# A hybrid decoder layer on one core: one more pair of up columns and two more down tiles by half products, raw chunks asked for one pair earlier, compression blocks laid out contiguously

## The chip, the cores and the metric

One core of a Trainium2 chip runs the whole layer as one program. The metric is the device time of one execution in microseconds, as the median of several runs. A difference under 0.3% is about what a measurement of this kernel cannot tell from no change.

## The reference, cut to what matters

One decoder layer on 512 tokens of width 1024, in float32:

```python
h = rms_norm(x, mix_norm_g)
u, q, kv, nsa_g, merge_g = split(h @ w_in)
y_pool = pooling_mixer(u) @ w_pool_out          # windowed means of widths 2, 4, 8, 16
# compress_blocks: 31 blocks of 32 tokens, stride 16, for k and for v
blk = kv[:, idx] + pe
hid = silu(einsum('bnlgd,ldh->bngh', blk, w1)); kc = einsum('bngh,hd->bngd', hid, w2)
y_nsa = nsa_mixer(q, kv, ...) @ w_nsa_out       # compressed, selected and window attention
x = x + (gate_pool * y_pool + gate_nsa * y_nsa) @ w_out
h = rms_norm(x, ffn_norm_g)
gate_pre, val = split(h @ w_up)                 # 1024 -> 2 * 2816
x = x + (silu(causal_dwconv(gate_pre) + b) * val) @ w_down
```

The width 2816 is 22 tiles of 128 columns. Pair f below means tile f of gate and tile f of value.

## The kernel before, in words

**Numbers.** Every matrix product is made of three matmuls: a float32 operand is split into a high part (rounded to fp32r by ScalarE) and a low part (the rest), and high·high, high·low and low·high are summed in PSUM. Two kinds of split exist: `split` (ScalarE rounds, VectorE subtracts) and `split_by_dma` (ScalarE writes the negative, a DMA issued by GpSimd adds the raw values onto it, ScalarE rounds). The latter's transfers are called accumulates here; they are the rows `sl<-r`, `sl<-s`, `sl<-wraw`, `wlo<-wraw`, `tl<-tb`.

**Stages.** First q, k (`round_a`), then attention (stream `m`) with the feature products, pooling and pool_out (stream `f`) put between its matmuls; then `wno`, `out` (8 outputs `x2[f]`), and the feed-forward part. In attention's stage the compressed keys and values are made: for k and v, GpSimd adds the position terms (`kcb`), the sum is split into `kcs`, and 32 matmuls `tr<-w1s,kcs` multiply 16 block offsets by `w1`. Offset l of the 32 takes every eighth element of `kcs` as its stationary operand.

**Feed-forward.** Pairs 0 to 3 (`PLAIN = 4`) are plain: 2 x 8 x 3 matmuls with 512 columns. Pairs 4 to 21 go by half products: `seven` makes seven operands from four raw quarters of the two weight tiles (a11, a12 and five sums h1 to h5), and seven products of 4 x 3 matmuls with 256 columns each (`product`) take the place of eight. The moving side needs sums too: `halves` makes `nh`, `nl`, `th`, `tl` from `x2` once, after pair 0. A pair leaves its last two products (h5, h4) to be done after a11 of the next pair (`held`). Between the products stand pieces of the down product: groups of four y tiles (`dn_group`, started at the pairs in `AT`, handed out by `FILL`). One piece is 4 x 3 matmuls of 512 columns. The last six y tiles (16 to 21) are multiplied by half products at the end: four row pairs (`seven_into`, called dz below), 7 x 3 x 3 matmuls each, whose moving operands `zh`, `zl` are sums of y tiles (`sums_of`).

**What sets the order.** Everything is recorded as operations with dependencies; a planner (`Plan.run`) gives each engine an order by costs and due times, tries several and keeps the best by its own `TRIALS`. Engines then work through their orders strictly. 56 pages of 512 columns hold most tiles. Pages taken by `soon` (raw chunks r1 and r2, the sums s3, the halves sh and sl) are given in a fixed sequence, the order in which the program asks for them, and such a page is taken only if `AHEAD` pages are free. Weight chunks go through a ring of three `wraw` buffers. SyncE (SP) issues all loads, GpSimd (POOL) all accumulates.

Nearly all instructions are recorded at one helper line (L398), so rows are told apart by tile names.

Of the kernel before, what the change touches and what calls it, by code (L numbers as in the profile page):

```python
# [15 lines left out]
P = 128  # L16
# [29 lines left out]
_o = 0  # L46
for _n, _w in (("ident", 128), ("mask", 512), ("cmask", 128), ("valid", 4), ("recip", 64), ("inv", 8)):
# [12 lines left out]
TRIES = 12  # L60
# [51 lines left out]
class Plan:  # L112
# [116 lines left out]

    def run(self, key, reserve, land, rate=RATE, fixed=None):  # L230
        ops = self.ops
# [33 lines left out]
        def settle(limit):  # L265
            while True:
                act = [l for l in queue.values() if l and l[0][0] <= now[0]]
                t = min((l[0][0] for l in queue.values() if l and l[0][0] > now[0]), default=1e18)
                head = None
                if act:  # L270
                    l = min(act, key=lambda l: l[0][1])
                    if now[0] + l[0][1] * len(act) <= t:
                        t, head = now[0] + l[0][1] * len(act), l
                if t > limit:
                    return False
                for l in act:
                    l[0][1] -= (t - now[0]) / len(act)
                now[0] = t
                if head:
                    o = head.pop(0)[2]  # L280
                    o.fin = t + land
                    finish(o)
                    return True
# [95 lines left out]
    def emit(self, tries, reserve):  # L379
# [8 lines left out]
        for i in range(tries):  # L388
# [3 lines left out]
            fixed = {e: [o for o in order if o.eng == e] for e in ("PE", "ACT", "DVE", "POOL", "SP")}  # L392
            spans = sum(self.run(key, 0, land, rate, fixed)[1] for land, rate in TRIALS)
            if best is None or spans < best[0]:
# [7 lines left out]
def hybrid_layer(ctx: ExitStack, tc: tile.TileContext, first, xT, pos, par, cst, poolw, w1, wa, wb, wf,  # L402
# [162 lines left out]
    for k in range(KD):  # L565
# [180 lines left out]
    with pl.on("f"):  # L746
        for i in range(2):
# [6 lines left out]
            for a in range(2):  # L754
                b = page("kcb", (P, 2, 32, 8))
                POOL.tensor_add(b.rearrange("p g n l -> p (g n) l"), kc.rearrange("p g (n l) -> p (g n) l", l=8),
                                pe[:, i, 8 * a:8 * a + 8][:, None, :].to_broadcast([P, 64, 8]))
                KC[i, a] = pl.tile(sb, (P, 2, T), F32R, "kcs", ("ptc", "t_cst")[a], 1)
                split(KC[i, a][:, 0], KC[i, a][:, 1], b.rearrange("p g n l -> p (g n l)"))
        def pool_in(gi):  # L760
# [82 lines left out]
    for i in range(2):  # L843
# [264 lines left out]

    def seven(w, row, first, second, when):
        rg, r1, r2 = ring("wraw")[:, :2 * w], soon("r1")[:, :w], soon("r2")[:, :w]  # L1110
        SP.dma_start(rg, row)
        with pl.behind(*when):
            SP.dma_start(r1, first)
            SP.dma_start(r2, second)

        def pair():
# [6 lines left out]

        a1 = ring("whi", F32R)[:, :2 * w], ring("wlo", F32R)[:, :2 * w]
        split(*a1, rg)
        s3 = soon("s3")[:, :w]
        DVE.tensor_add(s3, rg[:, :w], r1)
        h5 = summed(r2)
        DVE.tensor_add(r1, r1, r2)
        h3 = summed(s3)  # L1130
        DVE.tensor_add(rg[:, :w], rg[:, :w], r1)
        h1 = summed(r1)
        h2 = pair()
        split(*h2, rg[:, :w])
        DVE.tensor_add(rg[:, w:], rg[:, w:], rg[:, :w])
        h4 = summed(rg[:, w:])
        return [tuple(q[:, i * w:(i + 1) * w] for q in a1) for i in range(2)] + [h1, h2, h3, h4, h5]

    def seven_into(o0, o1, w, mv, nk, done, last):
# [11 lines left out]
        def rest():  # L1151
            bq = any_bank()
            product(bq, h1, mv(2, 0), True, nk)
            add(o1, HI, bq, -1)
            product(bx, a12, mv(1, 0), False, nk)
            add(o0, LO, bx, 1)
            product(by, h2, mv(2, 1), False, nk)
            add(o0, HI, by, 1)
            product(bq, h4, mv(1, 1), False, nk)
            add(o0, HI, bq, 1)  # L1160
            done(0)
            product(by, h3, mv(3, 0), False, nk)
            add(o1, HI, by, -1)
            done(1)

            def end():
                product(by, h5, mv(3, 1), False, nk)
                add(o1, LO, by, -1)
                done(2)

# [29 lines left out]
    def take(f):  # L1200
# [20 lines left out]

    turn[0] = 16
# [4 lines left out]
    tt = [pl.tile(sb, (P, 2, T), F32R, "th", "ptc", 1)]   # L1227
    tt = [tt[0][:, k] for k in range(2)] + [page("th", dt=F32R) for _ in range(2)]
    t2 = pl.tile(sb, (P, 2, T), F32R, "th", "t_cst", 1)
    t2 = [t2[:, k] for k in range(2)] + [page("th", dt=F32R)]  # L1230
    t3 = [pl.tile(sb, (P, T), F32R, n, "t_" + n, 1) for n in ("oraw", "ot")]
# [25 lines left out]
    zh, zl, ylast = {}, {}, {}  # L1257

    def split_y(f, y):
        yh[f], yl[f] = page("yh", dt=F32R), page("yl", dt=F32R)  # L1260
        split(yh[f], yl[f], y)
        if f < 16:
            return
        ylast[f] = y
        if f % 2:
            k = (f - 16) // 2
            for i, x in enumerate(sums_of(ylast[f - 1], y)):
# [49 lines left out]
    def dn_group(g):  # L1317
        box = {}

        def load(c):  # L1320
            box[c] = weights(wdn[g, c].rearrange("p a k n -> p (a k n)"), 1024, "v")

        def part(pt, c, a, k0, k1):
            wh, wl = box[c]
            s = slice(a * 512, (a + 1) * 512)
            mm3(pt, wh[:, s], wl[:, s], yh, yl, 4 * g + k0, 4 * g + k1, koff=4 * g, nk=4 * g + 4, first=4 * g)

        def one(c, a, free):
            if a == 0:
                load(c)  # L1330
            pt = any_bank() if free else bank("sc", (P, 2, T))[:, 0]
            part(pt, c, a, 0, 4)
            DVE.tensor_add(x2[2 * c + a], pt, x2[2 * c + a])

        def both(free):
            load(0)
            pts = any_bank(), any_bank()
            for k0, k1 in ((0, 3), (3, 4)):
                for a in range(2):
# [9 lines left out]

    def up_fast(f, n1, n2, n3):  # L1350
        a11, a12, h1, h2, h3, h4, h5 = seven(512, flat(wup[f, 0]), flat(wup[f, 1, :, 0:4]), flat(wup[f, 1, :, 4:8]),
                                             begun[-2:-1])
        bx, by, bq = any_bank(), any_bank(), any_bank()
# [50 lines left out]
    fill(9, True)  # L1404
    def put(j, p):
        f = 2 * p + (j > 0)
        if p < 3 or j == 0:
            if j != 1:
                SP.dma_start(out[f], x2[f])
        else:  # L1410
            c = LO if j > 1 else HI
            SP.dma_start(out[f, :, c], x2[f][:, c])

    last = None
    for p in range(4):
        w7 = seven(384, flat(wdz[2 * p]), flat(wdz[2 * p + 1, :, 0:3]), flat(wdz[2 * p + 1, :, 3:6]), begun[-1:])
        last = seven_into(x2[2 * p], x2[2 * p + 1], w7, movy, 3, lambda j, p=p: put(j, p), last)
    last()
# [7 lines left out]
def _layout(x, positions, mix_norm_g, w_in, q_norm_g, k_norm_g, cmp_pe, cmp_w1, cmp_w2, pool_w,  # L1426
# [65 lines left out]
    wd = tiles(f(w_down)[0])  # L1492
    A["wdn"] = wd[:, :, :16].reshape(4, 2, P, 4, 4, P).transpose(3, 0, 2, 1, 4, 5)
    A["wdz"] = wd[:, :, [16, 18, 20, 17, 19, 21]]
    return {n_: np.ascontiguousarray(A[n_]) for n_ in _INS}
# [19 lines left out]
```

## Time and profile before

| | us |
|---|---|
| median of 3 runs (lowest to highest) | 691.58 (690.17 to 692.01) |
| the profiled execution | 692.38 |
| its span | 689.9 |
| TensorE busy | 681.9 (99%) |
| VectorE busy | 508.6 (74%) |
| ScalarE busy | 445.4 (65%) |
| GpSimd busy | 115.9 (17%) |

The span runs from the first to the last instruction of the profiled execution; 2.44 us of its time lie around it. Matmuls overlap in the records (one of 512 columns lasts 390 ns, and the next begins 227 ns later), so what one costs is read from the distance of starts. [...]

### The profile page before, as it was taken

The page shows a single profiled execution, that of the slowest core. Times are in us where ns is not written, and L with a number is a line of the kernel's source. Part 1 is how long each engine was busy: PE and PEld are TensorE (multiplying, and loading weights), DVE is VectorE, ACT ScalarE, POOL GpSimd, SP SyncE. Part 2 cuts the span into 40 slices and gives each one's busy share as a digit, 9 for nine tenths or more (in the row PEclk, how much of TensorE's full clock was granted, in tenths as well). Part 3 has the DMA queues.
Part 4 walks back from the last instruction along what each step waited for, and adds up shares of the span by engine and source line. Part 5 has one row for each costly group of instructions (what it writes and reads, how often), then busy time and mean ns, then how long its engine had stood idle before and what let it go on. Part 6 is the DMA issues. An engine that isn't in the chain of part 4 may idle for free.

```text
span 689.9 us, 11461 instructions
## 1 busy us (share of the span) xinstructions
PE 681.9 (99%) x4110; PEld 609.3 (88%) x4110; DVE 508.6 (74%) x1081; ACT 445.4 (65%) x835; POOL 115.9 (17%) x140
## 2 busy tenths in 40 slices
PE   9999999999999999999999999999999999999997
PEld 8898888888888888888888889999999989999897
DVE  7768868888888743876569966777767767778883
ACT  8566867777767653343467768777767756677751
POOL 0012210000000100000022223222212222111331
PEclk9999999999999999999999999999999999999999
DMA  8466975326546557734478878978867887856675
GB/s 300 143 169 178 278 200 151 97 76 152 123 97 178 136 152 245 277 123 138 138 169 225 176 178 174 217 162 192 188 162 191 201 196 188 179 123 141 150 168 123
DMA packets 49719, 118.19 MB, mean 171 GB/s; under 512 B 5760, under 2 KB 10496, under 8 KB 49664
## 3 DMA queue, kind: packets, MB, share of 16 engines
q1 hardware_dynamic: 31232, 77.36, 35.0%
q0 software_dynamic: 18144, 39.85, 32.3%
q8 instruction: 32, 0.52, 0.3%
q10 hardware_dynamic: 288, 0.27, 0.1%
q14 instruction: 23, 0.19, 0.1%
HBM read 70.27 MB, written 6.29 MB: 111 GB/s over the span
## 4 chain that ended last, share of the span: by engine, by line
PE 87%; DMA 5%; issue 4%; ACT 1%; DVE 1%; POOL 1%; POOLq 0%; ACTq 0%; DVEq 0%; SPq 0%
PE mm L398 38%; PE tr L398 28%; PE sc L398 11%; PE av L398 10%; DMA sl<-r 2%; DMA r<-wup 2%; DMA sl<-s 1%; POOL sl L398 1%; DMA x<-first 1%; DVE ft L398 0%; POOL tl L398 0%; ACT whi L398 0%; ACT ft L398 0%; ACT sl L398 0%; ACT sh L398 0%
## 5 line engine op out<-in xcount | busy, mean ns | idle before, releaser
L398 ACT ACTIVATE whi<-wraw 128x1024 fp32r<-128x1024 f32 (+1 forms) x91 | 93.4, 1028 | 53.3 <-issue 27.2
L398 DVE TENSOR_TENSOR wlo<-wraw,whi 128x1024 fp32r<-128x1024 f32 (+1 forms) x62 | 72.4, 1170 | 12.6 <-ACT whi L398 10.6
L398 POOL DMA_DIRECT2D wlo<-wraw x30 | 26.3, 875 | 324.9 <-ACT wlo L398 253.2
L398 PE MATMUL mm<-xh,whi 128*128 128x512 f32 x176 | 70.3, 399 | 0.1
L398 PE MATMUL mm<-xh,wlo 128*128 128x512 f32 x176 | 68.9, 392 | 0.0
L398 PE MATMUL mm<-xl,whi 128*128 128x512 f32 x176 | 68.8, 391 | 0.0
L398 POOL DMA_DIRECT2D sl<-r x44 | 38.0, 864 | 141.2 <-ACT sl L398 87.4
L398 PE MATMUL mm<-tl,sh 128*128 128x256 f32 x190 | 53.4, 281 | 0.0
L398 ACT ACTIVATE wlo<-wraw 128x1024 fp32r<-128x1024 f32 x30 | 31.7, 1059 | 32.5 <-PE mm L398 25.3
L398 PE MATMUL mm<-th,sh 128*128 128x256 f32 x174 | 49.2, 283 | 1.8 <-ACT u L398 1.8
L398 PE MATMUL mm<-th,sl 128*128 128x256 f32 x174 | 49.0, 282 | 0.0
L398 ACT ACTIVATE pp<-pp,asm 128x128 f32<-128x128 f32 (+3 forms) x64 | 35.6, 558 | 13.7 <-DVE asm L398 13.3
L398 PEld LDWEIGHTS mm<-xh,wlo 128*128 128x128 f32 x176 | 33.0, 188 | 7.3
L398 DVE SCALAR_TENSOR_TENSOR ft<-fg,pr,ft 128x511 f32<-128x511 f32 (+1 forms) x44 | 32.9, 749 | 7.7 <-ACT ft L398 7.0
L398 PEld LDWEIGHTS mm<-xh,whi 128*128 128x128 f32 x176 | 33.2, 189 | 5.6 <-DVE u L398 0.5
L398 PEld LDWEIGHTS mm<-xl,whi 128*128 128x128 f32 x176 | 33.1, 188 | 5.0
L398 PE MATMUL sc<-yh,whi 128*128 128x512 f32 x96 | 37.4, 390 | 0.0
L398 PE MATMUL sc<-yl,whi 128*128 128x512 f32 x96 | 37.4, 390 | 0.0
L398 PE MATMUL sc<-yh,wlo 128*128 128x512 f32 x96 | 37.3, 389 | 0.0
L398 PEld LDWEIGHTS mm<-tl,sh 128*128 128x128 f32 x190 | 35.8, 189 | 0.4
L398 PEld LDWEIGHTS mm<-th,sh 128*128 128x128 f32 x174 | 32.7, 188 | 3.2 <-ACT u L398 2.2
L398 ACT ACTIVATE sl<-r 128x512 fp32r<-128x512 f32 (+1 forms) x44 | 26.6, 603 | 10.7 <-DMA r<-wup 8.7
(435 smaller groups left out, 2184.7 us busy)
## 6 DMA issues: line engine op xcount, KB each, us to landing
wlo<-wraw POOLq DMA_DIRECT2D x30, 512.0 KB, 4.8
wraw<-wup SPq DMA_DIRECT2D x26, 512.0 KB, 4.0
wraw<-wf SPq DMA_DIRECT2D x22, 512.0 KB, 3.8
r<-wup SPq DMA_DIRECT2D x36, 256.0 KB, 5.8
sl<-r POOLq DMA_DIRECT2D x36, 256.0 KB, 5.8
wraw<-wdn SPq DMA_DIRECT2D x16, 512.0 KB, 4.0
sl<-s POOLq DMA_DIRECT2D x18, 256.0 KB, 6.1
sl<-wraw POOLq DMA_DIRECT2D x18, 256.0 KB, 5.2
```

The source lines that it names most:

```text
L398: getattr(self.real[o.eng], method)(*a, **kw)
```

## The change

`PLAIN` goes from 4 to 3, so pair 3 goes by half products too. The down groups take 3, 4, 4 and 3 tiles (`GROUPS`), and the last part takes eight tiles (14 to 21) instead of six, with four instead of three steps in each product; pieces of the first and last group are 9 matmuls. `seven` asks for r1 and r2 of the next pair before it asks for its own sums. The operands of pair 3 are made during `out` (`pre`), with pages of their own in place of the ring. Even y tiles of the last part keep only their lower half (`yq`). In `seven_into` the products stand in another order. The compression's `kcb` and `kcs` are laid out offset by offset, so that a stationary operand is 128 elements in a row. Pair 1's weights are split by VectorE, not by accumulates (`DIRECT`). The mask gets a buffer and a load of its own, whose space the feed-forward part uses again. The planner takes 0.7 us more for an accumulate to land, and asks for 2 free pages instead of 4.

```diff
-NCST = _o
+NCST = CST["mask"][0]
-PLAIN = 4
-DIRECT = (0, 3)
-AT = (4, 9, 13, 17)
+PLAIN = 3
+DIRECT = (0, 1, 3)
+GROUPS = (0, 3, 7, 11, 14)
+AT = (3, 8, 12, 16)
 FILL = {f: (0, 0, 0, 0) for f in range(22)}
-FILL.update({4: (0, 4, 0, 0), 5: (0, 1, 0, 0), 6: (0, 1, 0, 0), 7: (0, 1, 0, 0), 8: (0, 1, 0, 0)})
-FILL.update({f: (0, 1, 1, 0) for f in range(9, 18)})
-FILL.update({18: (0, 1, 0, 0), 19: (0, 1, 0, 0), 20: (0, 0, 0, 0), 21: (0, 0, 0, 0)})
+FILL.update({f: (0, 1, 0, 0) for f in range(3, 22)})
+FILL[3] = (0, 4, 0, 0)
+FILL.update({f: (0, 1, 1, 0) for f in range(8, 17)})
+FILL.update({20: (0, 0, 0, 0), 21: (0, 0, 0, 0)})
-TRIALS = ((0.6, RATE), (1.0, RATE), (1.6, RATE), (1.0, 0.9 * RATE))
-AHEAD = 4
+EXTRA = 0.7
+TRIALS = ((0.6, RATE, 0.0), (1.0, RATE, 1.5), (1.6, RATE, 0.5), (1.0, 0.9 * RATE, 1.0))
+AHEAD = 2
...
-                b = page("kcb", (P, 2, 32, 8))
-                POOL.tensor_add(b.rearrange("p g n l -> p (g n) l"), kc.rearrange("p g (n l) -> p (g n) l", l=8),
+                b = page("kcb", (P, 8, 64))
+                POOL.tensor_add(b.rearrange("p l x -> p x l"), kc.rearrange("p g (n l) -> p (g n) l", l=8),
                                 pe[:, i, 8 * a:8 * a + 8][:, None, :].to_broadcast([P, 64, 8]))
...
-                    PE.matmul(pt[0:m, 0:256], bass.AP(tensor=c.tensor, offset=c.offset + l // 8 * 8 + l % 8, ap=[list(c.ap[0]), [8, m]]),
+                    PE.matmul(pt[0:m, 0:256], c.rearrange("p l s x -> p (l s x)")[:, l % 8 * P + l // 8:l % 8 * P + P],
...
+    def raws(w, row, first, second, when):
+        r1, r2 = soon("r1")[:, :w], soon("r2")[:, :w]
         with pl.behind(*when):
             SP.dma_start(r1, first)
             SP.dma_start(r2, second)
+        return w, row, r1, r2
...
+    def seven(i, pre=False):
+        if not ahead:
+            ahead.append(raws_of(i))
+        w, row, r1, r2 = ahead.pop()
+        if pre:
+            rl, rh = soon("ra"), soon("rb")
+            with pl.behind(tail):
+                SP.dma_start(rl, row[:, :w])
+                SP.dma_start(rh, row[:, w:])
+        else:
+            rg = ring("wraw")[:, :2 * w]
+            SP.dma_start(rg, row)
+            rl, rh = rg[:, :w], rg[:, w:]
+        ahead.append(raws_of(i + 1))
...
             product(bq, h1, mv(2, 0), True, nk)
             add(o1, HI, bq, -1)
+            product(by, h2, mv(2, 1), False, nk)
+            add(o0, HI, by, 1)
             product(bx, a12, mv(1, 0), False, nk)
             add(o0, LO, bx, 1)
-            product(by, h2, mv(2, 1), False, nk)
-            add(o0, HI, by, 1)
+            done(0, LO)
+            product(by, h3, mv(3, 0), False, nk)
+            add(o1, HI, by, -1)
+            done(1, HI)
             product(bq, h4, mv(1, 1), False, nk)
             add(o0, HI, bq, 1)
-            done(0)
-            product(by, h3, mv(3, 0), False, nk)
-            add(o1, HI, by, -1)
-            done(1)
+            done(0, HI)
...
     for p in range(4):
+        if p == 2:
+            begun.append(tail)
+            pre[PLAIN] = seven(PLAIN, True)
...
-    A["wdz"] = wd[:, :, [16, 18, 20, 17, 19, 21]]
+    A["wdz"] = wd[:, :, [14, 16, 18, 20, 15, 17, 19, 21]]
```

**Place 1.** SP, in the middle of the up pairs, before: the loads of two pairs. A tile's number tells the order in which the program asked for it; `wraw` from `wup` is the pair's first weight tile, r1 and r2 are the two raw halves of its second.

```order
L398 DMA wraw_1315<-wup 128x1024
L398 DMA r1_1316<-wup 128x512
L398 DMA r2_1317<-wup 128x512
L398 DMA wraw_1337<-wdn 128x1024
L398 DMA wraw_1345<-wup 128x1024
L398 DMA r1_1346<-wup 128x512
L398 DMA r2_1347<-wup 128x512
```

The same place in the changed kernel:

```order
L401 DMA wraw_1218<-wup 128x1024
L401 DMA r1_1189<-wup 128x512
L401 DMA r2_1190<-wup 128x512
L401 DMA wraw_1240<-wdn 128x1024
L401 DMA wraw_1248<-wup 128x1024
L401 DMA r1_1219<-wup 128x512
L401 DMA r2_1220<-wup 128x512
```

On SP's queue r1 and r2 stand where they stood; what moved is their place in the sequence of pages (r1_1189 was asked for right after wraw_1188, one pair earlier). In the built program r1_1316 waits, among others, for the landing of the accumulate that reads r2_1287, a raw chunk of the pair before it; r1_1189 waits for the one that reads r1_1129, of two pairs before it.

**Place 2.** PE, last row pair, before: the end of the product with h3 (sh_1547) and the beginning of that with h5 (sh_1545), which writes the same bank tr_1555.

```order
L398 MATMUL tr_1555<-zh_1473,sh_1547 128x256
L398 MATMUL tr_1555<-zl_1474,sh_1547 128x256
L398 MATMUL tr_1555<-zh_1473,sl_1546 128x256
L398 MATMUL tr_1555<-zh_1378,sh_1545 128x256
L398 MATMUL tr_1555<-zl_1379,sh_1545 128x256
```

In the changed kernel, the end of h3 (sh_1565) and the beginning of what follows it:

```order
L401 MATMUL tr_1573<-zh_1494,sh_1565 128x256
L401 MATMUL tr_1573<-zl_1495,sh_1565 128x256
L401 MATMUL tr_1573<-zh_1494,sl_1564 128x256
L401 MATMUL mm_1574<-yh_1334,sh_1571 128x256
L401 MATMUL mm_1574<-yl_1335,sh_1571 128x256
```

The product with h4 (sh_1571, 12 matmuls into another bank) now stands between h3 and h5.

**Place 3.** DVE, from the gate of the last up pair (fg) to the first sum for the dz products (zl), before:

```order
L398 TENSOR_TENSOR fg_1457<-tr_1455,u1_1456 128x256
L398 SCALAR_TENSOR_TENSOR ft_1466<-fg_1457,pr_66,ft_1466 128x511
L398 SCALAR_TENSOR_TENSOR ft_1466<-fg_1457,pr_66,ft_1466 128x510
L398 TENSOR_TENSOR s3_1505<-wraw_1500,r1_1501 128x384
L398 TENSOR_TENSOR r1_1501<-r1_1501,r2_1502 128x384
L398 TENSOR_TENSOR wlo_1504<-wraw_1500,whi_1503 128x768
L398 SCALAR_TENSOR_TENSOR y_1458<-y_1458,ft_1466 128x512
L398 SCALAR_TENSOR_TENSOR ta_1469<-ta_1469,y_1458 128x256
L398 SCALAR_TENSOR_TENSOR tb_1470<-ta_1469,y_1458 128x256
L398 TENSOR_TENSOR yl_1468<-y_1458,yh_1467 128x512
L398 TENSOR_TENSOR zl_1472<-ta_1469,zh_1471 128x512
```

The same in the changed kernel:

```order
L401 TENSOR_TENSOR fg_1482<-mm_1480,u1_1481 128x256
L401 TENSOR_TENSOR yq_1485<-y_1452,yq_1485 128x256
L401 TENSOR_TENSOR sl_1514<-wraw_1501,sh_1513 128x512
L401 SCALAR_TENSOR_TENSOR ft_1487<-fg_1482,pr_66,ft_1487 128x511
L401 SCALAR_TENSOR_TENSOR ft_1487<-fg_1482,pr_66,ft_1487 128x510
L401 TENSOR_TENSOR s3_1525<-wraw_1520,r1_1502 128x512
L401 SCALAR_TENSOR_TENSOR y_1483<-y_1483,ft_1487 128x512
L401 SCALAR_TENSOR_TENSOR ta_1490<-ta_1490,y_1483 128x256
L401 TENSOR_TENSOR r1_1502<-r1_1502,r2_1503 128x512
L401 TENSOR_TENSOR zl_1493<-ta_1490,zh_1492 128x512
```

One other subtraction (s3) instead of three other instructions stands between the second `ft` and `y`. On PE, between the end of the last up pair and the first dz product, stand 18 matmuls of two pieces where there were 36 of three.

## Rows read from the trace of the kernel before

**Rows 1.** The page's sections 1 to 4, cut: the span, the busy times, the granted clock in 40 slices, the DMA queues (packets, MB, time of their packets as a share of 16 engines' span), the chain that ended last by engine.

```profile
span 689.9 us, 11461 instructions
PE 681.9 (99%) x4110; PEld 609.3 (88%) x4110; DVE 508.6 (74%) x1081; ACT 445.4 (65%) x835; POOL 115.9 (17%) x140
PEclk9999999999999999999999999999999999999999
...
q1 hardware_dynamic: 31232, 77.36, 35.0%
q0 software_dynamic: 18144, 39.85, 32.3%
...
PE 87%; DMA 5%; issue 4%; ACT 1%; DVE 1%; POOL 1%; POOLq 0%; ACTq 0%; DVEq 0%; SPq 0%
```

**Rows 2.** The timeline of PE at its four longest waits in the feed-forward part: the last matmul before, and the first after each (start us, us, engine, line, operation, tiles, shape; in brackets the idle time before it and what ended it).

```profile
412.59 0.28 PE L398 MATMUL tr<-ot,sh 128*128 128x256 f32 x1
413.70 0.39 PE L398 MATMUL tr<-th,sl 128*128 128x256 f32 x1 [0.83 <-DMA sl<-r]
...
564.90 0.28 PE L398 MATMUL av<-nh,wlo 128*128 128x256 f32 x1
566.34 0.39 PE L398 MATMUL mm<-th,sh 128*128 128x256 f32 x1 [1.16 <-ACT u L398]
...
632.40 0.28 PE L398 MATMUL tr<-nh,wlo 128*128 128x256 f32 x1
633.36 0.39 PE L398 MATMUL mm<-th,sh 128*128 128x256 f32 x1 [0.67 <-ACT u L398]
...
684.36 0.28 PE L398 MATMUL tr<-zh,sl 128*128 128x256 f32 x1
685.15 0.39 PE L398 MATMUL tr<-zh,sh 128*128 128x256 f32 x1 [0.51 <-DVE x L398]
```

**Rows 3.** The chain of waits in order of time (start us, us, what): one product of 12 matmuls with 256 columns, and one piece of the down product, 12 with 512.

```profile
419.41 1.42 PE mm L398 x12
420.83 2.73 PE sc L398 x12
```

**Rows 4.** Matmuls of the compression: all of them by tile (duration ns min/median/max), the weight loads of a contiguous operand of the same size in the groups by shape (busy us, mean ns), and from the chain of waits and PE's timeline the time that eight and four of them take (four end where the next row starts).

```profile
L398 PEld LDWEIGHTS tr<-w1s,kcs x32: 317/336/343, 76.4 to 90.7; 128*128 128x128 f32 x16, 128*127 128x127 f32 x16
L398 PEld LDWEIGHTS tr<-nh,sh 128*128 128x128 f32 x68 | 12.8, 188 | 0.0
76.81 1.82 PE tr L398 x8
85.61 1.81 PE tr L398 x8
79.84 1.00 PE L398 MATMUL tr<-w1s,kcs 128*127 128x256 f32 x4
80.68 0.39 PE L398 MATMUL mm<-xh,whi 128*128 128x512 f32 x1
```

**Rows 5.** The same stretch in windows: us, busy us of each engine (instructions), granted clock, mean busy share of the DMA engines, GB/s.

```profile
67.00:77.00 10.00, 10.00 (x52) 8.45 (x51) 8.99 (x27) 9.09 (x19) 4.31 (x4) 1.00 1.03 282
77.00:92.00 15.00, 15.00 (x70) 13.64 (x70) 9.74 (x24) 9.68 (x19) 1.64 (x3) 1.00 0.94 249
```

**Rows 6.** The chain of waits ahead of the first three waits of rows 2, and ScalarE's timeline ahead of the second.

```profile
404.56 9.10 DMA sl<-r
547.10 6.77 DMA sl<-r
554.00 5.73 DMA r<-wup
624.50 4.80 DMA sl<-s
560.39 0.63 ACT L398 ACTIVATE sl<-r 128x512 fp32r<-128x512 f32 x1 [2.24 <-DMA r<-wup]
```

**Rows 7.** The way into the dz products: PE's last matmul of the last up pair, then timelines of DVE and ACT, then PE's first matmul that needs the last z tile.

```profile
647.43 0.28 PE L398 MATMUL tr<-nh,sl 128*128 128x256 f32 x1
649.11 1.54 DVE L398 SCALAR_TENSOR_TENSOR ft<-fg,pr,ft 128x511 f32<-128x511 f32 x2 [0.93 <-ACT ft L398]
651.01 0.61 ACT L398 ACTIVATE ft<-ft 128x512 f32<-128x512 f32 x1
651.63 0.95 DVE L398 TENSOR_TENSOR wlo<-wraw,whi 128x768 fp32r<-128x768 f32 x1
652.50 0.68 DVE L398 SCALAR_TENSOR_TENSOR y<-y,ft 128x512 f32<-128x512 f32 x1
654.62 0.68 DVE L398 TENSOR_TENSOR zl<-ta,zh 128x512 fp32r<-128x512 f32 x1
657.50 0.28 PE L398 MATMUL av<-zh,sh 128*128 128x256 f32 x1
```

**Rows 8.** The way into the first half products: DVE's first use of the new norm, PE's first matmul of the first fast pair, the issues of the last accumulates of `halves` with their landing, and DVE's load in that stretch.

```profile
352.21 0.69 DVE L398 TENSOR_TENSOR fg<-av,rb 128x512 f32<-128x512 f32 x1 [1.83 <-ACT rb L398]
386.08 0.40 PE L398 MATMUL tr<-nh,whi 128*128 128x256 f32 x2
L398 POOL DMA_DIRECT2D tl<-tb x4: 859/862/1207, 358.3 to 394.8; - x4
DMA to landing us min/median/max: 3.3/5.7/7.4
341.00:394.00 53.00, 53.00 (x249) 44.40 (x248) 43.47 (x84) 39.55 (x61) 12.10 (x14) 1.00 0.78 182
```

**Rows 9.** Windows in the feed-forward part (columns as rows 5).

```profile
429.00:445.00 16.00, 16.00 (x127) 15.52 (x126) 11.31 (x18) 11.49 (x22) 3.66 (x5) 1.00 0.91 231
634.00:648.00 14.00, 14.00 (x107) 13.46 (x107) 12.55 (x24) 10.18 (x21) 2.80 (x4) 1.00 0.74 174
```

More of the change, by code (lines that the diff above doesn't have):

```diff
@@ L280, in settle @@
                     o = head.pop(0)[2]
-                    o.fin = t + land
+                    o.fin = t + land + (extra if o.eng == "POOL" else 0.0)
                     finish(o)
@@ L392, in emit @@
             fixed = {e: [o for o in order if o.eng == e] for e in ("PE", "ACT", "DVE", "POOL", "SP")}
-            spans = sum(self.run(key, 0, land, rate, fixed)[1] for land, rate in TRIALS)
+            spans = sum(self.run(key, 0, *trial, fixed)[1] for trial in TRIALS)
             if best is None or spans < best[0]:
@@ L1122, in summed @@
             return hi, lo
-        a1 = ring("whi", F32R)[:, :2 * w], ring("wlo", F32R)[:, :2 * w]
-        split(*a1, rg)
+        if pre:
+            a11, a12 = pair(), pair()
+            split(*a11, rl)
+            split(*a12, rh)
+        else:
+            a1 = ring("whi", F32R)[:, :2 * w], ring("wlo", F32R)[:, :2 * w]
+            split(*a1, rg)
+            a11, a12 = (tuple(q[:, i * w:(i + 1) * w] for q in a1) for i in range(2))
         s3 = soon("s3")[:, :w]
-        DVE.tensor_add(s3, rg[:, :w], r1)
+        DVE.tensor_add(s3, rl, r1)
         h5 = summed(r2)
@@ L1130, in seven @@
         h3 = summed(s3)
-        DVE.tensor_add(rg[:, :w], rg[:, :w], r1)
+        DVE.tensor_add(rl, rl, r1)
         h1 = summed(r1)
         h2 = pair()
[L1134 to L1137, printed above, removed]
+        split(*h2, rl)
+        DVE.tensor_add(rh, rh, rl)
+        h4 = summed(rh)
+        return [a11, a12, h1, h2, h3, h4, h5]
     def seven_into(o0, o1, w, mv, nk, done, last):
@@ L1168, in end @@
                 add(o1, LO, by, -1)
-                done(2)
+                done(1, LO)
             return end
@@ L1226, in hybrid_layer @@
     yh, yl = [None] * KF, [None] * KF
[L1227 to L1230, printed above, removed]
+    tt, t2 = ([x[:, 0], x[:, 1], y] for x, y in
+              ((pl.tile(sb, (P, 2, T), F32R, "th", n, 1), pl.tile(sb, (P, T), F32R, "th", "t_" + m, 1))
+               for n, m in (("ptc", "vst"), ("t_cst", "mask"))))
+    tt.append(page("th", dt=F32R))
     t3 = [pl.tile(sb, (P, T), F32R, n, "t_" + n, 1) for n in ("oraw", "ot")]
@@ L1257, in hybrid_layer @@
     zh, zl, ylast = {}, {}, {}
+    LAST = GROUPS[-1]
     def split_y(f, y):
+        ylast[f] = y
+        if f >= LAST and f % 2 == 0:
+            q = page("yq", dt=F32R)
+            yh[f], yl[f] = q[:, LO], q[:, HI]
+            split(yh[f], yl[f], y[:, LO])
+            return
         yh[f], yl[f] = page("yh", dt=F32R), page("yl", dt=F32R)
         split(yh[f], yl[f], y)
[L1262 to L1266, printed above, removed]
+        if f > LAST:
+            k = (f - LAST) // 2
             for i, x in enumerate(sums_of(ylast[f - 1], y)):
@@ L1304, in mov @@
         return tuple((lambda k, q=q: q[k, i - 2][:, half * H2:(half + 1) * H2]) for q in (th, tl))
-    held, begun, fills = [], [], []
+    held, fills = [], []
     def finish():
@@ L1337, in both @@
             pts = any_bank(), any_bank()
-            for k0, k1 in ((0, 3), (3, 4)):
+            for k0, k1 in ((0, n - 1), (n - 1, n)):
                 for a in range(2):
@@ L1350, in up_fast @@
     def up_fast(f, n1, n2, n3):
-        a11, a12, h1, h2, h3, h4, h5 = seven(512, flat(wup[f, 0]), flat(wup[f, 1, :, 0:4]), flat(wup[f, 1, :, 4:8]),
-                                             begun[-2:-1])
+        a11, a12, h1, h2, h3, h4, h5 = pre.get(f) or seven(f)
         bx, by, bq = any_bank(), any_bank(), any_bank()
@@ L1404, in hybrid_layer, with put @@
     fill(9, True)
[L1405 to L1411, printed above, removed]
+    def put(f, c):
+        if f > 5:
             SP.dma_start(out[f, :, c], x2[f][:, c])
+        elif c == (LO if f % 2 else HI):
+            SP.dma_start(out[f], x2[f])
     last = None
     for p in range(4):
-        w7 = seven(384, flat(wdz[2 * p]), flat(wdz[2 * p + 1, :, 0:3]), flat(wdz[2 * p + 1, :, 3:6]), begun[-1:])
-        last = seven_into(x2[2 * p], x2[2 * p + 1], w7, movy, 3, lambda j, p=p: put(j, p), last)
+        w7 = seven(KF + p)
+        last = seven_into(x2[2 * p], x2[2 * p + 1], w7, movy, 4, lambda i, c, p=p: put(2 * p + i, c), last)
     last()
```

42 lines of the change are left out of this document (26 added, 16 removed).

## The prediction

> **What bounds the kernel.** I read the page's busy times first, then the clock, the chain that ended last, the timeline of the busiest engine, and last the DMA shares. TensorE (PE) is busy in 99% of the span, the clock is granted at its full level in every slice, and the chain that ended last is 87% PE [rows 1]. So the time is PE's work plus PE's waits. Other engines, VectorE with 74% and ScalarE with 65% [rows 1], matter only where PE waits for them. The four longest waits of the feed-forward part are in PE's timeline: from the last matmul before to the first after, 413.70 − 412.59 = 1.11 us, 1.44, 0.96 and 0.79 [rows 2]. Starts of 256-column matmuls lie 1.42 / 12 = 0.118 us apart without a wait [rows 3], so the waits cost 0.99, 1.32, 0.84 and 0.67 us, 3.82 together.
>
> **The sum** is made against the profiled execution, 692.38 us (span 689.9 and 2.44 around it). It lies 0.80 above the median, 691.58, and at the end this is taken off.
>
> *Compression.* 32 matmuls take their stationary operand at a stride of eight elements; loading it takes 336 ns in the median, a contiguous one of the same size 188 ns [rows 4]. A matmul with 256 columns can't begin more often than its weights are loaded: eight take 1.82 and 1.81 us, and four take 80.68 − 79.84 = 0.84 [rows 4]. So 32 take 2 × 1.82 + 4 × 0.84 = 7.0 us, and at 0.118 they would take 3.8: **−3.2**. The bounds are −3.2 and nothing. Nothing, if something else sets the pace there: the DMA share is 1.03 and 0.94 in this stretch [rows 5]. I take the whole, since the slow loads stand in the records themselves. The price of the new layout is that GpSimd writes `kcb` with a stride; GpSimd is busy 17% [rows 1], and if `kcs` comes late for it, this is part of the same bound.
>
> *Products.* Pair 3 goes from 2 × 8 × 3 matmuls of 512 columns, four times 2.73, to seven products of 1.42 [rows 3]: 9.94 − 10.92 = −0.98. Two more down tiles go from 48 matmuls of 512 columns (4 × 2.73) to 84 of 256 (7 × 1.42): −0.98 again. **−2.0**. It is bounded by itself: these are counts times the pace PE keeps.
>
> *Raw chunks a pair sooner.* The wait of 1.32 at 564.9 goes back through the chain: the accumulate into `sl` begins at 547.10 and lands after 6.77, only then the load of the next raw chunk is issued, at 554.00, and lands after 5.73; ScalarE stood 2.24 us on it, with all that is behind it in its strict order [rows 6]. By place 1 the same chunk now waits for an accumulate of two pairs before, about 10 to 12 us sooner (a pair with a piece is 7 × 1.42 + 2.73 = 12.7), much more than 1.32. The wait of 0.84 at 632.4 ends a chain through the accumulate into `sl` from a sum, issued at 624.50, 4.80 to land [rows 6], which the same lateness feeds. **−2.2** for both, between 0 and this. What is late next on this path is the weight tile through the `wraw` ring; its place on SP hasn't moved.
>
> *The first fast pair.* The wait of 0.99 at 412.6 is on an `sl` accumulate that took 9.10 us, issued among the last ones of the `halves` [rows 6]. With pair 3's operands made during `out`, its accumulates are long done. **−1.0**. What hides this work: seven VectorE operations of 0.68 each [rows 7], 4.8 us, in a stage some 40 us long; if they were in nobody's shadow this would cost 4.8. The other additions (VectorE 14 instructions, ScalarE 13, GpSimd 2 in all, and a second load for the mask) have a quarter of VectorE's span and a third of ScalarE's to hide in [rows 1]; pair 1's split on VectorE lies under four pieces of 2.73.
>
> *The last row pair.* The wait of 0.67 at 684.4 is for a VectorE subtraction that must read the bank before h5 overwrites it [rows 2]. By place 2, h4 (1.42) now stands between; the subtraction is done by then: **−0.7**, bounds 0 and this.
>
> *What is late next: the entry of the row pairs.* From the last matmul of the last up pair, 647.43, plus 0.12, to the end of the last `zl`, 654.62 + 0.68, is 7.75 us; the chain on VectorE is held 0.87 by the `wlo` between silu (651.01) and y (652.50) [rows 7]. Now this time has less cover: 18 matmuls of two pieces (18 × 0.227 = 4.1), a11 (1.42) and three quarters of h1 (1.07), 6.6 us. If the chain stays, PE waits 1.15; place 3 shows the `wlo` gone from this place, which leaves 6.9 and a wait of 0.3. I take **+0.3**, bounds 0 and 1.15.
>
> *And the entry of the half products.* VectorE first uses the new norm at 352.21, PE's first half product came at 386.08 [rows 8]. It comes four pieces (10.9) sooner, at 375.2. Then 1.42 of a11, 36 matmuls of the down group (8.2), h1, h2 and a12 (4.3) and 1.07, until the fourth `tl` is needed at about 390. In the changed order 53 VectorE instructions stand from 352.2 to the one that feeds it; at the mean of this stretch, 43.47 / 84 = 0.52 [rows 8], they take 28 us, and some 3 us of waits bring this to 383.5. The accumulate lands 3.3 to 7.4 us later (median 5.7) [rows 8], at 387 to 391 after its issue: between 3 us early and 1.3 late. I take **+0.7**, bounds 0 and 1.3, because the accumulates of pairs crowd there.
>
> 692.4 − 3.2 − 2.0 − 2.2 − 1.0 − 0.7 + 0.3 + 0.7 = 684.3, and less 0.8: 683.5.
>
> **Rivals.** *The DMA engines become the bound (the slower side).* q1 moves 77.36 MB in 35.0% of the span, 3.12 us of all sixteen engines per MB; q0, the accumulates, 39.85 MB in 32.3%, 5.59 per MB [rows 1]. A half-product pair loads 1.05 MB and accumulates 1.05 MB: 3.3 + 5.9 = 9.1 us, and PE needs 9.94 where no piece stands in the pair. There are six such pairs now: 20, 21 and four row pairs. If the sixteen engines can't be kept busier than a share s, a pair takes 9.13 / s. At 0.75 this is 12.2, five times 2.2 us more (the last pair has no successor): 694.7. My gain is gone at s = 0.79, and it is slower by more than 0.3% (2.1 us, about what a measurement of this kernel can tell from no change) below 0.76. For it: the stretch before the row pairs, the last pairs without pieces, shows a share of 0.74 with PE waiting [rows 9]. Against it: 0.91 over 16 us in the middle with PE never idle [rows 9], and the row pairs of before stood in the same proportion (0.79 MB twice, 6.9 us, to 7 × 1.07 = 7.5 of PE) and ended with the one bank wait of rows 2. [...]
>
> [...]
>
> *The raw chunks don't come sooner in effect.* On SP's queue they stand where they stood; if what is ahead of them there holds them, the waits of 1.32 and 0.84 stay, and with both entries at their far ends, 2.45 instead of 1.0, the sum is 683.5 + 2.2 + 1.45 = 687.1. For it: SP is strictly in order, and `wraw` before them waits for its ring. Against: at 554.0 it was the accumulate that was late, not the ring [rows 6].
>
> *The compression keeps its time*, since DMA is full there [rows 5]: 683.5 + 3.2 = 686.7. Against: 32 loads at 336 ns in the records, whose minimum is 317 [rows 4]: with a stride none was fast.
>
> **Chances.** The forecast 0.64, DMA as bound 0.12, raw chunks no sooner 0.15, compression unchanged 0.09. **683.5 us.** Low end: no new waits (−1.0), and of the 8.0 us in which PE was idle over the whole span [rows 1] the new order takes up to 1.5 more: 681.0. High end: above 686.7 and 687.1 with as much of a margin as the new waits have on their own, 688.0; beyond it lies the DMA rival, and little else. Faster by more than 0.3%: all but the DMA rival, and a little of that, 0.89; within: 0.06; slower: 0.05.
>
> **What would show it.** PE: 72 more matmuls (168 more of 256 columns, 96 fewer of 512), and a busy time about 5 lower. Compression: weight loads near 188 ns, eight matmuls in about 0.95. Middle: no PE wait on `sh` or ScalarE's `sl<-r` over half a microsecond; the load of r landing a pair before its use. Entries: PE's idle before the fourth `th` or `tl` product and before the first `zl`, both under 1.3. Last row pair: no PE wait on VectorE's `x`. The prediction is wrong if PE's idle time in pairs 20 to the end exceeds 2 us with DMA shares above 0.9 (the rival), or if new waits of the same kind appear elsewhere, where the planner's other order has less slack than I read.

## The result and the profile after

| | before | after |
|---|---|---|
| median of 6 runs each (us) | 691.50 (690.17 to 692.20) | 687.58 (687.07 to 688.42) |
| ratio, 95% interval | | 0.9946 (0.9934 to 0.9959) |
| the profiled execution | 692.38 | 687.15 |
| its span | 689.9 | 685.2 |

The change saves 3.9 us where 8.0 were forecast, and 687.58 lies inside the range, near its upper end. The direction was right and half of the gain is missing. Two executions far out, 1743.44 us of the kernel before and 2388.96 us of `combined`, are left out of the ratios below.

The page of the changed kernel, the lines that answer to [rows 1], and below them the issues of one kind of accumulate (KB each, median us to landing):

```profile
span 685.2 us, 11656 instructions
PE 677.8 (99%) x4182; PEld 608.9 (89%) x4182; DVE 515.5 (75%) x1095; ACT 451.7 (66%) x848; POOL 117.4 (17%) x142
PEclk9999999999999999999999999999999999999999
...
q1 hardware_dynamic: 31808, 77.36, 34.4%
q0 software_dynamic: 18432, 40.90, 33.7%
...
PE 93%; DMA 4%; issue 1%; DVE 1%; ACT 0%; POOL 0%; POOLq 0%; ACTq 0%
...
sl<-r POOLq DMA_DIRECT2D x46, 256.0 KB, 4.3
```

PE has 72 records more, as the counts said. None of the four waits of [rows 2] is left. PE's timeline in pair 21 (the last up pair), and its longest wait in the row pairs, shows what is there now:

```profile
619.06 0.40 PE L401 MATMUL tr<-nh,whi 128*128 128x256 f32 x2
619.29 0.28 PE L401 MATMUL tr<-nh,wlo 128*128 128x256 f32 x1
622.40 0.58 PE L401 MATMUL tr<-th,sh 128*128 128x256 f32 x1 [2.82 <-ACT u L401]
622.77 0.41 PE L401 MATMUL tr<-tl,sh 128*128 128x256 f32 x1
...
653.56 0.39 PE L401 MATMUL mm<-zh,sl 128*128 128x256 f32 x1 [0.17 <-DMA sl<-r]
```

One wait takes 622.40 − 619.29 = 3.11 us from start to start, 2.99 more than the pace of 0.118; the four of before took 3.82 together. It is not the whole price. The windows around it (columns as [rows 5]; the last three are granted clock, DMA share, GB/s):

```profile
608.00:616.00 8.00, 8.00 (x70) 8.00 (x70) 6.77 (x12) 4.68 (x11) 2.39 (x3) 1.00 0.88 191
616.00:619.40 3.40, 3.40 (x31) 3.37 (x29) 0.38 (x1) 1.75 (x3) 0.00 (x0) 1.00 0.62 111
619.40:622.40 3.00, 0.18 (x3) 0.01 (x1) 2.17 (x5) 2.38 (x7) 0.86 (x1) 0.94 0.43 76
622.40:625.40 3.00, 3.00 (x14) 3.00 (x15) 1.52 (x5) 2.07 (x5) 0.86 (x1) 0.50 0.38 66
```

Behind the idle stretch the granted clock is 0.50 for three microseconds. The chain of waits has the price, and where it begins (its first two rows are the compression's):

```profile
76.43 0.95 PE tr L401 x8
...
78.76 0.48 PE tr L401 x4
...
609.64 1.42 PE av L401 x12
611.73 5.82 DMA sl<-r
622.40 2.93 PE tr L401 x12
625.32 1.55 PE av L401 x12
```

Twelve matmuls that take 1.42 elsewhere take 2.93, and the next twelve 1.55: 1.64 us more. So the place costs 2.99 + 1.64 = 4.6 us. It begins with an accumulate issued at 611.73 that lands 5.82 later. ScalarE's timeline there:

```profile
612.86 0.63 ACT L401 ACTIVATE sl<-s 128x512 fp32r<-128x512 f32 x1
617.65 0.63 ACT L401 ACTIVATE sh<-s 128x512 fp32r<-128x512 f32 x1 [4.17 <-DMA sl<-r]
618.19 0.80 ACT L401 ACTIVATE ft<-fg,pr 128x512 f32<-128x512 f32 x1
...
621.97 0.37 ACT L401 ACTIVATE u<-tr 128x256 f32<-128x256 f32 x1
```

The rounding `sh<-s` (of s3, for h3) has its input long before. It waits for an accumulate of another operand: `sl<-r`, which reads the raw chunk r2 for h5. No data lead from one to the other. In the built program `sh_1471` lies at the address of `r2_1433`: it was given the page of r2, and that page is free when the accumulate has read it. Behind it on ScalarE's strict order stands `u<-tr`, the copy that empties PE's bank, and PE waits for that.

### The profile page after: what moved, and what is told of

The parts are those of the page before. It is cut to its first block, busy times and chain, and to the rows that moved or that the text cites. A ratio compares the mean times of both kernels' runs of the same rounds, so it can differ in the third digit from the quotient of the medians.

```text
span 685.2 us, 11656 instructions
## 1 busy us (share of the span) xinstructions
PE 677.8 (99%) x4182; PEld 608.9 (89%) x4182; DVE 515.5 (75%) x1095; ACT 451.7 (66%) x848; POOL 117.4 (17%) x142
## 4 chain that ended last, share of the span: by engine, by line
PE 93%; DMA 4%; issue 1%; DVE 1%; ACT 0%; POOL 0%; POOLq 0%; ACTq 0%
PE mm L401 37%; PE tr L401 32%; PE sc L401 13%; PE av L401 12%; DMA sl<-r 4%; DMA x<-first 0%; POOL sl L401 0%; DVE ft L401 0%; ACT ft L401 0%; DVE th L401 0%; DVE u L401 0%; ACT sl L401 0%; ACT sh L401 0%; ACT xh L401 0%; DVE fg L401 0%
## 5 line engine op out<-in xcount | busy, mean ns | idle before, releaser
L401 ACT ACTIVATE whi<-wraw 128x1024 fp32r<-128x1024 f32 (+1 forms) x89 | 90.6, 1019 | 66.2 <-issue 26.8
L401 POOL DMA_DIRECT2D sl<-r x46 | 40.0, 869 | 229.5 <-ACT sl L401 217.8
L401 PE MATMUL tr<-nh,whi 128*128 128x256 f32 x216 | 46.6, 282 | 0.0
L401 ACT ACTIVATE wlo<-wraw 128x1024 fp32r<-128x1024 f32 x28 | 29.6, 1059 | 24.4 <-PE mm L401 23.7
L401 PE MATMUL tr<-nh,wlo 128*128 128x256 f32 x144 | 40.5, 281 | 0.0
L401 PEld LDWEIGHTS tr<-nh,whi 128*128 128x128 f32 x216 | 35.6, 188 | 0.0
L401 PE MATMUL sc<-yh,whi 128*128 128x512 f32 x91 | 35.5, 390 | 0.0
L401 PE MATMUL tr<-th,sh 128*128 128x256 f32 x104 | 29.8, 287 | 2.8 <-ACT u L401 2.8
L401 PE MATMUL tr<-tl,sh 128*128 128x256 f32 x113 | 32.3, 286 | 0.0
L401 ACT ACTIVATE sl<-r 128x512 fp32r<-128x512 f32 x46 | 28.7, 623 | 5.5 <-DMA sl<-r 3.1
```

What stands on the lines that cost most here:

```text
L401: getattr(self.real[o.eng], method)(*a, **kw)
```

## The experiments

Differences are to the median of the runs of the kernel before on the same chip, measured beside it.

**A page apart for the tile that waited.** The wait could be one of pages, or of DMA engines that can't keep up (the prediction's slower rival).

```diff
-        h3 = summed(s3)
+        h3 = summed(s3, i == 21)
+            lo, hi = soon("sl", F32R)[:, :w], (other() if apart else soon("sh", F32R))[:, :w]
```

(`other` gives a tile in the space of `rb`; the plan of the order still counts it as a page.)

> The changed kernel with every engine's instructions in the same order; only the tile sh of the sum s3 of up pair 21 lies in the space of a constant that is no longer read (rb) instead of in one of the 56 pages. In the changed kernel this sh was given the page of r2 of the same pair, which an accumulate was still reading (issued at 611.73, ScalarE stood 4.17 us on it, PE 2.98 + 0.26 us at 622.4 behind ScalarE). Theory 1, the pages ran out: ScalarE's stall and PE's wait go, 3.2 us less than the changed kernel, about 684.4. Theory 2, the DMA engines can't carry pairs without pieces: the accumulates land as late as before, PE waits 2 to 3 us at 622 or a little later, and the time stays within 1 us of 687.6.

686.66 against 689.94, ratio 0.9941 (0.9925 to 0.9956): as the changed kernel. Timelines of VectorE, ScalarE and PE:

```profile
615.27 0.42 DVE L401 TENSOR_TENSOR fg<-mm,u 128x256 f32<-128x256 f32 x1
619.25 0.43 DVE L401 TENSOR_TENSOR ta<-y 128x256 f32<-128x256 f32 x1 [3.56 <-DMA sl<-r]
621.55 0.63 ACT L401 ACTIVATE ft<-ft 128x512 f32<-128x512 f32 x1 [3.97 <-DVE ft L401]
623.29 0.39 PE L401 MATMUL tr<-th,sh 128*128 128x256 f32 x1 [2.44 <-ACT u L401]
```

The number of theory 1 failed, and so did a single page as the remedy. `sh<-s` no longer waits; now VectorE's `ta<-y`, the next tile that asks for a page, waits 3.56 us on the same accumulate, since it inherits r2's page (in the built program `ta_1456` waits for it). ScalarE then waits for VectorE and PE for ScalarE. By itself this run can't tell "more than one page is missing" from "DMA is too slow".

**The accumulate taken away, order of PE unchanged.**

```diff
-        h5 = summed(r2)
+        h5 = summed(r2, i == 21)
+            if own:
+                hi, lo = pair()
+                split(hi, lo, x)
+                return hi, lo
```

(`own` is the second argument; `split` rounds on ScalarE and subtracts on VectorE. On PE every instruction stands where it stood; on ScalarE, VectorE and SP the planner moved a few, from about 574 us on.)

> The changed kernel, but in up pair 21 alone the low part of h5 is made by a VectorE subtraction instead of an accumulate by DMA, so that the page of r2 is free about 1.5 us after ScalarE's rounding, not 6; the planner makes its order anew. Theory (one accumulate of 5.9 us holds a page that the next tile in line needs, and with all 56 pages taken any next tile inherits it): PE's wait in pair 21 falls below 1 us and the lower clock behind it goes too, 3 to 4.4 us less than the changed kernel. Rival (the DMA engines as a whole can't keep up in pairs 20 and 21): PE waits as long on the accumulates of h3 or h1, no more than 1 us is won.

> The kernel own_split_21 once more beside the others of this call: 7.5 us under before, within 1.

682.71 against 690.25, ratio 0.9893 (0.9865 to 0.9921), and again 682.93 against 691.13, 0.9891 (0.9865 to 0.9916): 7.5 and 8.2 us under before, and 4.0 under the changed kernel measured beside it (`after_again`, 686.75). ScalarE in this place:

```profile
612.95 0.63 ACT L401 ACTIVATE sl<-s 128x512 fp32r<-128x512 f32 x1
613.91 0.64 ACT L401 ACTIVATE sh<-s 128x512 fp32r<-128x512 f32 x1 [0.33 <-PE mm L401]
```

and the window in which PE had waited:

```profile
616.00:622.40 6.40, 6.40 (x57) 6.40 (x56) 4.85 (x10) 5.39 (x11) 1.72 (x2) 1.00 0.52 106
```

`sh<-s` comes 3.7 us sooner, PE is not idle in this window, the clock stays. In the profile of `own_split_again` PE has one wait, later, in the row pairs, on another accumulate:

```profile
648.86 0.39 PE L401 MATMUL mm<-zh,sl 128*128 128x256 f32 x1 [0.98 <-DMA sl<-r]
```

So waits on accumulates are not gone altogether. And the edit took away 256 KB of DMA work as well as the hold on the page.

**The DMA work put back, without the page.** Two instructions are put into the finished order of `own_split_21`, so nothing else moves:

```diff
+                idle = pool_tile(sb, (P, T), F32, "idle", "t_rb")
+                pl.extra = {pl.ops[-2].i: [("memset", (idle, 0.0), {}),
+                                           ("dma_start", (idle[:, :w], f32(hi)), {"accum_op": ALU.add})]}
```

> The kernel own_split_21 with every engine's order kept and two instructions more on GpSimd in pair 21: a tile in the space of rb is set to zero, and an accumulate of 256 KB adds the rounded r2 onto it at the place where the accumulate of h5 stood in the changed kernel. So the DMA engines have the same work as in the changed kernel, and no page of r2 is held by it; the added tile is read by nobody. Theory (the held page): as own_split_21, 7.5 under before, PE without a wait of over 0.5 us in pair 21. Rival (the amount of DMA work): the wait of 2.5 to 3 us is back, with the lower clock behind it, 3.5 to 3.9 under before.

683.79 against 691.13, ratio 0.9905 (0.9882 to 0.9928): 7.3 under before. GpSimd, ScalarE, and the windows:

```profile
612.32 0.86 POOL L403 DMA_DIRECT2D idle<-sh  x1 [2.77 <-ACT yq L401]
614.30 0.64 ACT L401 ACTIVATE sh<-s 128x512 fp32r<-128x512 f32 x1 [0.33 <-PE mm L401]
```

```profile
608.00:616.00 8.00, 8.00 (x70) 8.00 (x69) 7.55 (x14) 6.18 (x13) 3.12 (x4) 1.00 0.78 185
612.00:618.00 6.00, 6.00 (x53) 6.00 (x52) 5.59 (x11) 3.94 (x8) 2.58 (x3) 1.00 0.97 241
616.00:622.00 6.00, 6.00 (x50) 5.78 (x49) 4.10 (x9) 4.47 (x11) 1.34 (x2) 1.00 0.60 106
```

The added accumulate runs where the old one ran, lands 5.1 us after its issue, and nobody waits for it. While it is under way the DMA engines are as full as they were in the changed kernel in this stretch:

```profile
612.00:618.00 6.00, 6.00 (x54) 6.00 (x52) 2.81 (x7) 1.52 (x4) 1.45 (x2) 1.00 0.98 220
```

So the amount of DMA work by itself did not make the wait; what the accumulate held did. By the medians the work costs 0.9 us (683.79 to 682.93), within the spread of the runs.

**Raw chunks in their own turn, in the changed kernel.**

```diff
-        ahead.append(raws_of(i + 1))
```

> The changed kernel, but seven asks for r1 and r2 of a pair in that pair's own turn, as the kernel before did. Theory, asking a pair sooner is what took away the waits on raw chunks (2.2 us together): one or two waits of ScalarE on r<-wup of over 1 us, PE behind them. Since two pages fewer are held, the page wait of 3.2 at pair 21 may go at the same time: 686.6 if it does, 689.8 if it stays. Rival, the earlier asking did nothing: no wait on r<-wup, and the time is 687.6 or, without the page wait, 684.4.

> Both: raw chunks asked in their own turn as in the kernel before, and h5 of pair 21 split by VectorE. Theory A, asking a pair sooner is worth what the kernel late_raws showed as waits on raw chunks and at the entry of the row pairs (1.46 + 0.62 + 0.94 us): 1 to 3 us slower than own_split_21, 4.5 to 6.5 under before. Theory B, it is worth nothing: the same as own_split_21, 7.5 under before.

`late_raws`: 684.50 against 689.94, ratio 0.9916 (0.9901 to 0.9931), 5.4 under before, where the changed kernel was 3.9 and 3.5 under (the result above and `after_again`): 1.5 to 1.9 faster. SP, ScalarE and PE:

```profile
609.67 1.48 SPq L401 DMA_DIRECT2D r<-wup  x2
615.27 0.63 ACT L401 ACTIVATE sl<-r 128x512 fp32r<-128x512 f32 x1 [2.81 <-DMA r<-wup]
619.85 0.39 PE L401 MATMUL tr<-th,sh 128*128 128x256 f32 x1 [1.30 <-ACT u L401]
640.78 0.39 PE L401 MATMUL mm<-zl,sh 128*128 128x256 f32 x1 [0.35 <-DVE zl L401]
650.81 0.39 PE L401 MATMUL mm<-zh,sl 128*128 128x256 f32 x1 [0.77 <-DMA sl<-r]
```

Both halves of the expectation came: the wait on r2's page is gone, and a wait on raw chunks is back (2.81 on ScalarE, 1.30 on PE), so the earlier asking does take that away. It takes away less than it costs. With pair 21's h5 split by VectorE, late raw chunks give 683.85 against 691.13, 0.9898 (0.9876 to 0.9919), beside 682.93: asking sooner is then worth 0.9 us by the medians, which these runs can't tell from nothing. ScalarE's waits on raw chunks in the kernel before (first row), and in `late_own_21` these and PE's longest wait in the feed-forward part (total us, times, longest):

```profile
ACT sl L398 <- DMA r<-wup: 8.7, 6, 3.3
ACT sl L401 <- DMA r<-wup: 22.9, 8, 4.2
PE mm L401 <- DVE zl L401: 0.3, 1, 0.3
```

In the changed kernel ScalarE has no such wait. So the earlier asking does on ScalarE all that it should, but hardly any of the 22.9 us reaches PE without it. In both of these runs the planner also made much of the other order anew.

**More at once**, beside the edit of `own_split_21`:

```diff
-PAGES = 56
+PAGES = 57
-AHEAD = 2
+AHEAD = 3
-    rb = keep("rb", (P, T))
+    rb = page("rb")
-        ahead.append(raws_of(i + 1))
+        if i >= 20:
+            ahead.append(raws_of(i + 1))
```

> The changed kernel with raw chunks asked a pair sooner only from pair 20 on, with one more page (the constant rb, read until 372 us, becomes a page like the others), AHEAD 3, and h5 of pair 21 split by VectorE. Theory: what cost time was pages held too long, not the amount of DMA work; none of the waits of over 1 us is left in the up pairs, and the time lies 6 to 8 us under before. Rival (the DMA engines are the bound): no better than the kernel with late raw chunks, 5.4 us under before.

683.71 against 690.25, 0.9902 (0.9868 to 0.9936): inside what was expected, and no better than `own_split_21`. With that one page freed in time, a further page and later loads bring nothing that could be measured. No profile shows whether waits of over 1 us are left in its up pairs.

**The compression alone, in the kernel before.** The change's own lines on `kcb` and `kcs`, and

```diff
-bass.AP(tensor=c.tensor, offset=c.offset + l // 8 * 8 + l % 8, ap=[list(c.ap[0]), [8, m]]),
+c.rearrange("p l s x -> p (l s x)")[:, l % 8 * P + l // 8:l % 8 * P + P],
```

> The kernel before with the contiguous compression blocks alone, order of instructions unchanged. Theory, the stride is what slows the weight loads: loads near 188 ns, eight matmuls in 0.95 us in place of 1.82, 3.2 us less than before, about 688.3. Rival, DMA or something else sets the pace there, or the chain that follows is late anyway: 691.5, loads faster or not.

686.48 against 689.94, ratio 0.9949 (0.9933 to 0.9965), 3.5 under before. All loads of the group, by tile:

```profile
L398 PEld LDWEIGHTS tr<-w1s,kcs x32: 187/188/191, 75.7 to 86.9; 128*128 128x128 f32 x16, 128*127 128x127 f32 x16
```

The 336 ns of [rows 4] have become 188, and the slowest of the 32, 191, lies below the fastest there. No run shows why the step of eight float32 costs this.

**The order in the row pairs, in the kernel before.** First h4 moved behind h3, which put h3 right behind h2 into the same bank; then (`row_pair_order`) h2 moved ahead of a12 as well, as in the changed kernel.

```diff
             product(by, h2, mv(2, 1), False, nk)
             add(o0, HI, by, 1)
-            product(bq, h4, mv(1, 1), False, nk)
-            add(o0, HI, bq, 1)
-            done(0)
             product(by, h3, mv(3, 0), False, nk)
             add(o1, HI, by, -1)
+            product(bq, h4, mv(1, 1), False, nk)
+            add(o0, HI, bq, 1)
+            done(0)
             done(1)
```

> The kernel before with the product of h4 between h3 and h5 in the four row pairs, nothing else. Theory, PE's wait of 0.67 us at 684.4 is for VectorE to read the bank before h5 overwrites it: gone, 0.7 less, about 690.8. Rival, the wait moves to another place of the row pairs: 691.5.

692.36 against 689.94, ratio 1.0034 (1.0023 to 1.0044): 2.4 slower. PE:

```profile
657.39 0.39 PE L398 MATMUL tr<-zh,sh 128*128 128x256 f32 x1 [0.58 <-DVE x L398]
665.63 0.39 PE L398 MATMUL tr<-zh,sh 128*128 128x256 f32 x1 [0.51 <-DVE x L398]
673.86 0.39 PE L398 MATMUL tr<-zh,sh 128*128 128x256 f32 x1 [0.51 <-DVE x L398]
682.10 0.39 PE L398 MATMUL tr<-zh,sh 128*128 128x256 f32 x1 [0.51 <-DVE x L398]
```

My edit made the wait four times instead of removing it once: from start to start 0.74 and three times 0.68 for a product that follows another into its bank, 2.8 in all and 2.1 more than the one wait of before. The planner moved instructions of other engines from the start on, and the DMA waits of [rows 2] don't stand in this profile, so that 2.1 lies near the 2.4 is no proof that the bank explains all of it.

> The kernel before with the products of the four row pairs in the order of the changed kernel (h1, h2, a12, h3, h4, then h5 in the next pair), nothing else, so that no product stands right behind another into the same bank. Theory: the 0.68 us wait at the end goes and none of the four that came with h3 right behind h2 appears: 0.7 less than before. Rival: the planner's order moves other waits by as much, no difference.

689.28 against 690.25, ratio 0.9987 (0.9971 to 1.0002). No wait on `x` is left in its trace; the time fits 0.7 but the interval reaches to no change.

**The same kernels once more.**

> The changed kernel once more, beside the three others of this call and the same runs of the kernel before. If the wait of PE in pair 21 belongs to the order and the pages, it is there again, 2.5 to 3.5 us, with a matmul stretch at the lower clock behind it, and the difference to before is again near 3.9. If it was chance of one execution, it is gone and the difference is larger.

> The kernel before once more, for its profile: are PE's waits of 0.99, 1.32 and 0.84 us on accumulates and raw chunks a property of the kernel or of one execution? If of the kernel, all three are there within 0.3 us. If of the execution, some are missing or other ones appear, their sum differs by more than 1 us from 3.15, and the span goes with it.

`after_again`: 686.75 against 690.25, ratio 0.9965 (0.9945 to 0.9985). PE waits in the same place:

```profile
622.04 0.46 PE L401 MATMUL tr<-th,sh 128*128 128x256 f32 x1 [2.37 <-ACT u L401]
```

It belongs to the kernel. The three DMA waits of before change from one execution to the next. PE's waits in `before_again` (690.10):

```profile
413.50 0.39 PE L398 MATMUL tr<-th,sl 128*128 128x256 f32 x1 [1.23 <-DMA sl<-r]
565.43 0.39 PE L398 MATMUL mm<-th,sh 128*128 128x256 f32 x1 [0.45 <-ACT u L398]
683.36 0.39 PE L398 MATMUL tr<-zh,sh 128*128 128x256 f32 x1 [0.51 <-DVE x L398]
```

and in `compress_alone`, which has the instructions of before in the same order (its last wait, as in before, is the bank of the row pairs):

```profile
560.78 0.39 PE L398 MATMUL mm<-th,sh 128*128 128x256 f32 x1 [0.49 <-ACT u L398]
```

Start to start, the first three places of [rows 2] cost 0.99 + 1.32 + 0.84 = 3.15 in the execution that I read, 1.39 + 0.61 = 2.00 in the second, 0.65 in the third. The wait on the bank, 0.68, is there each time.

## Why the prediction was off, point by point

**Compression: right.** Predicted −3.2. In the chain the 32 matmuls now take 0.95 for eight and 0.48 for four, 2 × 0.95 + 4 × 0.48 = 3.8 where [rows 4] gave 7.0; alone the edit brought 3.5.

**Products: right.** −2.0 predicted from counts and pace. What all distances of PE's starts differ from their pace (the median for each number of columns), summed, is 14.3 us before and 11.7 after; the span less this is 675.6 and 673.5, 2.1 apart. This shows that the pace was kept; no run has this edit alone.

**The last row pair: right, small.** The wait is gone in the changed kernel; the order alone gave 1.0, with an interval from 2.0 less to 0.1 more, so its price is not shown by a time.

**The entries: right in part.** I took 0.3 for the row pairs and 0.7 for the half products. Start to start, 0.15 stands at the first row pair, and nothing at the first half product; 0.33 at the second row pair is a wait on an accumulate that I had not listed. My upper bound for the half products was added up wrongly as well: 383.5 + 7.4 is 390.9, and 375.2 + 1.42 + 8.2 + 4.3 + 1.07 is 390.2, so it was 0.7 and not 1.3.

**Raw chunks a pair sooner: the step that failed.** I priced this edit by the wait that it removes (−2.2) and looked for what is late next on its own path, the `wraw` ring. What it takes I put at nothing, without a reason: two pages more, held through a whole pair. In pair 21 a page that an accumulate was still reading went to the next tile in line. Whichever got it, `sh` in the changed kernel, `ta` in `spare_page`, had to wait until that transfer of 5.8 us had landed, and strict order carried the wait through ScalarE to PE. Costs: 2.99 of waiting and 1.64 at the lower clock, 4.6 us where the step said −2.2 and no price. The gain was too large, too: the waits that made up the 2.2 measure 0.61 and 0.65 in two other executions of the same order, and with pair 21 repaired the earlier asking is worth 0.9 by the medians. The prediction named the case only in its last sentence (a planner's order with less slack than read) and gave it no chance of its own.

**The DMA rival: its sign came, its mechanism did not.** It stood for this place, a pair without pieces, and the sign that I had named for it was met: PE idle for more than 2 us from pair 20 on (2.82 and 0.17), with a DMA share above 0.9 (0.98 from 612 to 618, while the accumulate was under way). But its price needed engines that can't be kept busier than 0.79. And in `own_split_traffic`, with the same traffic and a share of 0.97 in the same stretch, PE is busy throughout. The sign was too weak: it could not tell a wait for a page from a wait for DMA engines. How far the full engines lengthened the transfer that held the page was not told apart. A wait on a DMA is not yet a shortage of DMA.

**An amount counted twice.** I took 3.15 us of DMA waits from one execution at their full size, and then another 0.8 off because that execution lay above the median. It lay there, at least in part, by these same waits: 2.00 and 0.65 in others of the same order. The profiled run of the changed kernel lies 0.4 below its median.

Together, on the median: 683.5 + 4.6 (pair 21) − 0.5 (entries cheaper than taken) + 0.8 (counted twice) = 688.4, against 687.58; the 0.8 between them is not accounted for. With pair 21 repaired, the changes give −7.5 and −8.2, near the −8.0 of the forecast. This does not confirm the terms: that kernel has one accumulate less, and `late_own_21`, without the earlier asking, comes to −7.3. Part of the agreement is luck.

**Open.** The last group of eight tiles keeps more y and z tiles than the six before, and the raw chunks two pages. The planner also asks for 2 free pages instead of 4. That the accumulate's hold on a page makes the wait is shown; which of these uses up the pages was not told apart. For the earlier asking `late_raws` speaks, where the page wait is gone, but the planner made the rest of its order anew too. Why this accumulate takes 5.8 us, when the median of its kind is 4.3, was not tried.

## What to carry to other kernels

When loads are moved forward, price the buffers that they hold as well as the wait that they end: ask which tile inherits a buffer last read by a slow transfer, and what stands behind that tile on its engine. Where a releaser has no data for the waiting instruction, ask whether the wait is for space. Here `sh<-s` stood 4.17 us in such a wait; a faster releaser in the one place where it mattered ended it, and one buffer more only passed it on (3.56 us on VectorE in `spare_page`). Take waits on transfers from several executions before they go into a sum, and never correct for the median a second time.

## What the hardware showed that I had not expected

PE idle for 2.8 us was followed by three microseconds at a granted clock of 0.50, so that a wait of 3.0 us cost 4.6. After the 1.30 us of idle in `late_raws`, which ended at 619.85, the clock stayed; its window right behind:

```profile
620.00:622.00 2.00, 2.00 (x18) 2.00 (x19) 1.97 (x5) 1.98 (x5) 0.21 (x2) 1.00 1.05 182
```

And in the row pairs a product that begins in the PSUM bank of the product right before it cost 0.68 to 0.74 us, four times in `h4_between` and once in the kernel before; each time PE waited for VectorE's `x`, which reads the bank.
